# State-space decays as a product of running sums, and the stage's Pool work on DVE

## The chip, the cores and the metric

The kernel runs on one core of one Trainium2 chip. What is measured is the device time of one launch in microseconds. Of the kernel before there are three runs: 1285.94, 1286.4 and 1287.54 us, median 1286.4 us. The engines are called PE (matmul; PEld is its weight load), DVE (vector), ACT (scalar), POOL and SP, which issues most DMAs.

## The reference, cut to what matters

Two transformer blocks over 256 tokens of width 1024. The second block has a sparse attention, a state-space (SSD) branch and a mixture of experts. The change lies in the SSD branch, and there in the decay between two tokens of one chunk:

```python
dt = softplus(dt_raw + dt_bias); A = -exp(a_log)
a_cs = cumsum(dt * A)                        # along the tokens of a chunk
seg = a_cs[:, :, :, None] - a_cs[:, :, None, :]
decay = exp(where(causal, seg, -inf))        # one per head, token l, token s <= l
cb = einsum('bclgn,bcsgn->bclsg', C, B)
y_diag = einsum('bclsg,bclsgr,bcsgrp->bclgrp', cb, decay, x * dt)
...
y = y_diag + y_off + d_skip[:, None] * x
```

There are 32 heads of width 64 in 4 groups of 8.

## The kernel before

Everything is unrolled in one program. In order of time: a feed-forward layer and a mixer (to about 400 us), the second feed-forward layer (to about 600 us), a gated input (`ple`), then `block2` (about 640 to 1022 us), the routing (to about 1050 us) and the experts, whose weights stream in until the end. Large products are made of three fp32r matmuls each (`mm3`, L207 to L209; `xbc`, L1023 to L1025): every weight tile arrives by DMA as `raw`, ACT rounds it to `hi` (L190) and DVE takes the rest `lo = raw - hi` (L191). So each weight tile costs ACT and DVE an instruction before PE can use it.

The kernel's tiles work on two halves of 128 tokens (t = 0, 1), and the SSD chunk here is such a half. `block2` first makes the attention, and `steps` (L1050) the step sizes `dt` and `da = dt * A` (128 tokens x 2 halves x 32 heads), with `das`, `da` split into two fp32r parts (L1066, L1067). `overlaps` (L1075) makes the products of B and C, masked by `tri`. Then `ssd` (L1128) runs over eight units (g, t), and `weave` (L1210) puts steps of a filler between its parts: the `xbc` products of the next groups with their convolutions (`conv_pair`, L982, whose taps are DVE instructions at L991 and L999), the gates and the attention's output product. Per unit:

- `weights(g, t)` (L1086): POOL scales the triangle `tri` by each of 8 heads' `das`, once for each part, giving two tiles `ra` of 128 x 1024 (L1091). PE multiplies them by `upper_r` (L1097, L1098), which sums `da` between two tokens, for 4 heads at a time into one PSUM bank; ACT takes the exponential into `M` (L1099) and DVE multiplies by the masked overlaps (L1100). DVE makes `xdt` (L1105); POOL makes the skip term `ys` (L1106) and, for t = 0, `xw` (L1110).
- `take(g, t)` (L1112): for t = 1 the product with the state (L1118), scaled by DVE (`yo`, L1120) and added to `y` by POOL (L1121); the 16 matmuls of `M` and `xdt` (L1125) and the sum on DVE (L1126).
- `gated(g, t)` (L1144): the gate and a normalisation, whose power is taken on POOL (`rstd`, L138) between DVE instructions (L136, L140, L141, L143).

Each engine runs its own list of instructions in order. The lists of PE, DVE, ACT and SP are set by a planner before the launch, which follows the program's order as a priority and takes later instructions ahead where their inputs are there (`steps` runs at 665 us on DVE, for instance). POOL's list is the program's order (`manual_schedule`), so a normalisation's power stands behind the `ra` of the unit that the program names before it. Work tiles come from pools of slots by size (25 of 4 KB a partition, 7 of 2 KB, 8 of 1 KB); a tile waits for a free slot.

`block2_consts` (L817) has its first part after the mixer, with the masks on POOL, its second in the middle of the last products of the second feed-forward layer (`between`, about 592 us), where DVE copies `upper` to `upper_r` (L837).

Of the kernel before, what the change touches and what calls it, by code (L numbers as in the profile page):

```python
# [54 lines left out]
def tile_blocks(ctx, tc, a, out):  # L55
# [43 lines left out]
    def bc(ap, shape):  # L99
        return ap.to_broadcast(shape)  # L100
# [716 lines left out]
    def block2_consts():  # L817
        cs2 = cp.tile([128, 2, 2, 8], F32, name="cs2")
        sn2 = cp.tile([128, 2, 2, 8], F32, name="sn2")
        for t in range(2):  # L820
            G.dma_start(cs2[:, t].rearrange("p j d -> p (j d)"), a["c_cos2"][t * 128:(t + 1) * 128, :])
            G.dma_start(sn2[:, t].rearrange("p j d -> p (j d)"), a["c_sin2"][t * 128:(t + 1) * 128, :])
        g_q = row_bcast(a["q_norm_2"], 64, "g_q2")
        g_k = row_bcast(a["k_norm_2"], 64, "g_k2")
        g_ik = row_bcast(a["idx_k_norm_2"], 64, "g_ik2")
        b_dt = row_bcast(a["dt_bias_2"], 32, "b_dt")
        a_neg = row_bcast(a["a_log_2"], 32, "a_neg")
        d_row = row_bcast(a["d_skip_2"], 32, "d_row")
        tri = select_mask(F32, "tri", (1.0, 0.0), ALU.is_ge, 0, -1, 1)
        upper = select_mask(F32, "upper", (1.0, 0.0), ALU.is_gt, 0, 1, -1)  # L830

        cw_in = heap([120, 128], name="cw_in")
        G.dma_start(cw_in[:96, :], a["conv_w_2"].rearrange("j (b f) -> (j b) f", f=128))
        G.dma_start(cw_in[96:120, :], a["conv_b_2"].rearrange("(b f) -> b f", f=128))
        yield
        upper_r = cp.tile([128, 128], FR, name="upper_r")
        keep(V.tensor_copy(upper_r, upper))  # L837
        cw = cp.tile([128, 5, 24], F32, name="cw")
        p = tp()
        keep(PE.transpose(p[:, 0, :120], cw_in, ident[:120, :120]))  # L840
        V.tensor_scalar(cw.rearrange("p j b -> p (j b)"), p[:, 0, :120], 0.5, None, op0=ALU.mult)
        keep(S.activation(a_neg, a_neg, AF.Exp))
        V.tensor_scalar(a_neg, a_neg, -1.0, None, op0=ALU.mult)
        wn = heap([128, 8, 104], name="wn")
        for c0, n0, n in ((0, 2048, 72), (72, 7240, 32)):
            nc.sync.dma_start(wn[:, :, c0:c0 + n], w_src(a["w_in_2"], 0, 8, n0, n))
        yield
        wh, wl = heap([128, 8, 104], FR, name="wnh"), heap([128, 8, 104], FR, name="wnl")
        keep(S.copy(wh, wn))
        V.tensor_tensor(wl, wn, wh.bitcast(F32), op=ALU.subtract)  # L850
        yield cs2, sn2, g_q, g_k, g_ik, b_dt, a_neg, d_row, tri, upper, upper_r, cw, wh, wl

    def block2(x, px, consts, done):
        w_in = a["w_in_2"]
        cs2, sn2, g_q, g_k, g_ik, b_dt, a_neg, d_row, tri, upper, upper_r, cw, wh, wl = consts

        sx = px.x

# [174 lines left out]
        dtx = small([128, 2, 32], name="dtx")  # L1033
        dt = small([128, 2, 32], name="dt")
        da = small([128, 2, 32], name="da")
        das = [small([128, 2, 32], FR, name="das") for _ in range(2)]

        def narrow():

# [6 lines left out]
                yield True  # L1046

        dec = small([128, 2, 32], name="dec")

        def steps():  # L1050

            e, s2, pl = [small([128, 2, 32], name="sps") for _ in range(3)]
            V.scalar_tensor_tensor(e, dtx, -1.0, dtx, op0=ALU.mult, op1=ALU.min)
            S.activation(e, e, AF.Exp)
            V.tensor_scalar(pl, e, 2.0, None, op0=ALU.add)
            V.reciprocal(pl, pl)
            V.tensor_tensor(e, e, pl, op=ALU.mult)
            V.tensor_tensor(s2, e, e, op=ALU.mult)
            V.tensor_scalar(pl, s2, 1.0 / 17, None, op0=ALU.mult)
            for n in (15, 13, 11, 9, 7, 5, 3):  # L1060
                V.scalar_tensor_tensor(pl, pl, 1.0 / n, s2, op0=ALU.add, op1=ALU.mult)
            V.scalar_tensor_tensor(pl, pl, 1.0, e, op0=ALU.add, op1=ALU.mult)
            V.tensor_scalar(dtx, dtx, 0.0, None, op0=ALU.max)
            V.scalar_tensor_tensor(dt, pl, 2.0, dtx, op0=ALU.mult, op1=ALU.add)
            V.tensor_tensor(da, dt, bc(a_neg[:, None, :], [128, 2, 32]), op=ALU.mult)
            V.tensor_copy(das[0], da)  # L1066
            V.tensor_tensor(das[1], da, das[0].bitcast(F32), op=ALU.subtract)  # L1067
            pe_ = at((128, 2, 32))
            PE.matmul(pe_[:, 0, :], upper, da[:, 0, :], start=True, stop=False)
            PE.matmul(pe_[:, 1, :], tri, da[:, 1, :], start=False, stop=True)  # L1070
            S.activation(dec, pe_, AF.Exp)
# [14 lines left out]
        def weights(g, t):  # L1086

            hs = slice(g * 8, g * 8 + 8)
            ra = [heap([128, 8, 128], FR, name="ra") for _ in range(2)]
            for i in range(2):  # L1090
                G.tensor_tensor(out=ra[i], in0=bc(tri[:, None, :], [128, 8, 128]),  # L1091
                                in1=bc(das[i][:, t, hs, None].bitcast(F32), [128, 8, 128]), op=ALU.mult)
            M = heap([128, 8, 128], name="M")
            for i in range(2):
                h4 = slice(4 * i, 4 * i + 4)
                ps = at((128, 4, 128))
                PE.matmul(ps, upper_r, ra[0][:, h4, :], start=True, stop=False)  # L1097
                PE.matmul(ps, upper_r, ra[1][:, h4, :], start=False, stop=True)  # L1098
                S.activation(M[:, h4, :], ps, AF.Exp)  # L1099
                V.tensor_tensor(M[:, h4, :], M[:, h4, :], bc(state["cb"][0][:, g, None, t, :], [128, 4, 128]), op=ALU.mult)  # L1100
            if t == 0:
                ys[g] = heap([128, 2, 8, 64], name="y")
            xv = xs[g][:, t, :].rearrange("p (h d) -> p h d", d=64)
            xdt = heap([128, 8, 64], name="xdt")
            V.tensor_tensor(xdt, xv, bc(dt[:, t, hs, None], [128, 8, 64]), op=ALU.mult)  # L1105
            G.tensor_tensor(out=ys[g][:, t], in0=xv, in1=bc(d_row[:, hs, None], [128, 8, 64]), op=ALU.mult)  # L1106
            state[g, t] = M, xdt
            if t == 0:
                xw = state[g] = heap([128, 8, 64], name="xw")
                G.tensor_tensor(out=xw, in0=xdt, in1=bc(dec[:, 0, hs, None], [128, 8, 64]), op=ALU.mult)  # L1110

        def take(g, t):  # L1112
            hs = slice(g * 8, g * 8 + 8)
# [2 lines left out]
            if t == 1:  # L1116
                pof = at((128, 8, 64))
                PE.matmul(pof, state["cb"][1][:, g, :], state[g], start=True, stop=True)  # L1118
                yo = heap([128, 8, 64], name="yo")
                V.tensor_tensor(yo, pof, bc(dec[:, 1, hs, None], [128, 8, 64]), op=ALU.mult)  # L1120
                G.tensor_tensor(out=y, in0=y, in1=yo, op=ALU.add)  # L1121
            py = mm((128, 8, 64), "o")
            for i in range(8):
                for c in (slice(0, 64), slice(64, 128)):
# [553 lines left out]
```

## Time and profile before

| | us |
|---|---|
| median of three runs | 1286.4 |
| the profiled execution | 1286.94 |
| its span in the profile | 1285.2 |
| `block2` with the SSD units | 800 to 970 |
| its last products | 970 to 1022 |
| routing, experts | 1022 to 1285 |

The rows further down are of the profiled execution, whose times run from the span's start. A line number is the line of the kernel that issued the instruction, which can be a helper's. The granted clock (PEclk) is TensorE's share of full speed. Busy times of one engine are joined; idle time of an engine that nobody waits for costs nothing.

### The profile page before, as it was taken

To read this page: it belongs to the slowest core of one execution; us is meant where nothing else is said; L and a number is where in the kernel's file an instruction comes from. 1 tells how busy PE (TensorE), PEld (TensorE's weight loads), DVE (VectorE), ACT (ScalarE), POOL (GpSimd) and SP (SyncE) were. 2 spreads that over 40 slices of the span, in tenths; PEclk is the share of its full clock that TensorE was granted. 3 is DMA by queue.
4 is the path that set the end of the run, shared out by engine and by line. 5 is a ranking of instruction groups with operands and counts; after the bars stand their busy time and mean duration, and the time that the engine had idled before them with its cause. 6 is when DMAs were issued, how large, how long until landed. Compare 5 with 4: busy or idle time off the path is not lost.

```text
span 1285.2 us, 19517 instructions
## 1 busy us (share of the span) xinstructions
PE 1194.2 (93%) x7806; PEld 956.8 (74%) x7807; DVE 759.3 (59%) x1313; ACT 547.6 (43%) x842; POOL 130.9 (10%) x146
## 2 busy tenths in 40 slices
PE   7999999989999999999998899989999979787886
PEld 6999989977777999987777788877778855342421
DVE  5555648675466656646778777998785652121212
ACT  5444535456664444435554666455533321010100
POOL 2000001120002200000001100533430010000000
PEclk9999999999999999999999999999999979999998
DMA  9553655463335654656444244344546859999995
GB/s 335 172 195 121 240 166 169 152 204 136 108 115 169 190 196 141 219 182 193 164 144 151 99 132 134 129 139 124 126 170 214 317 226 391 408 409 408 409 409 201
DMA packets 105567, 266.83 MB, mean 208 GB/s; under 512 B 8580, under 2 KB 15920, under 8 KB 105472
## 3 DMA queue, kind: packets, MB, share of 16 engines
q1 hardware_dynamic: 103488, 260.50, 57.7%
q0 software_dynamic: 1840, 4.52, 1.3%
q8 instruction: 63, 1.03, 0.3%
q10 hardware_dynamic: 144, 0.52, 0.1%
q14 instruction: 32, 0.26, 0.1%
HBM read 264.47 MB, written 1.05 MB: 207 GB/s over the span
## 4 chain that ended last, share of the span: by engine, by line
PE 44%; DMA 13%; DVE 11%; issue 7%; POOL 2%; ACT 1%; SPq 0%; DVEq 0%; POOLq 0%; ACTq 0%
PE mm L207 6%; PE mm L209 6%; PE mm L208 6%; DMA wq<-in_w_up_dram 4%; DVE lo L191 4%; DMA wq<-in_w_down_dram 3%; DMA wq<-in_w_gate_dram 3%; PE mm L261 2%; PE mm L262 2%; PE mm L260 2%; PE at L261 2%; PE at L262 2%; PE at L260 2%; POOL r L138 1%; PE at L1467 1%
## 5 line engine op out<-in xcount | busy, mean ns | idle before, releaser
L191 DVE TENSOR_TENSOR lo<-raw,hi 128x1024 fp32r<-128x1024 f32 (+3 forms) x312 | 374.4, 1205 | 213.2 <-ACT hi L190 209.8
L190 ACT CAST hi<-raw 128x1024 fp32r<-128x1024 f32 (+3 forms) x312 | 315.6, 1015 | 338.6 <-PE o L208 93.8
L138 POOL TENSOR_TENSOR r<-ms,phalf 128x1 f32<-128x1 f32 (+2 forms) x40 | 38.8, 969 | 715.1 <-DVE ms L136 709.9
L1467 PE MATMUL at<-wq,xg 128*32 128x256 f32 x736 | 67.0, 402 | 17.4 <-DMA wq<-in_w_up_dram 13.1
L207 PE MATMUL mm<-hi,xah 128*128 128x512 f32 x192 | 78.8, 410 | 2.9 <-DVE zs L1162 2.9
L209 PE MATMUL mm<-hi,xal 128*128 128x512 f32 x192 | 76.4, 398 | 0.3 <-DVE xal L163 0.3
L208 PE MATMUL mm<-lo,xah 128*128 128x512 f32 x192 | 76.3, 398 | 0.2 <-DVE ms L136 0.2
L1467 PEld LDWEIGHTS at<-wq,xg 128*32 128x32 f32 x736 | 30.0, 114 | 47.9 <-DMA wq<-in_w_up_dram 23.8
L1477 DVE SCALAR_TENSOR_TENSOR act<-at,cg,sa 128x256 f32<-128x256 f32 x8 | 5.3, 666 | 92.6 <-ACT sa L1474 92.5
L1023 PE MATMUL mm<-xah,hi 128*128 128x256 f32 x192 | 56.8, 296 | 3.2 <-ACT sq L892 3.2
L1024 PE MATMUL mm<-xal,hi 128*128 128x256 f32 x192 | 55.0, 286 | 0.0
L1025 PE MATMUL mm<-xah,lo 128*128 128x256 f32 x192 | 55.0, 286 | 0.0
L1474 ACT ACTIVATE sa<-at,rs 128x256 f32<-128x256 f32 x8 | 3.8, 473 | 116.0 <-PE at L1467 77.7
L262 PE MATMUL mm<-x1h,lo 128*128 128x256 f32 x176 | 50.9, 290 | 1.1 <-DVE lo L191 1.1
L261 PE MATMUL mm<-x2l,hi 128*128 128x256 f32 x176 | 50.7, 288 | 1.1 <-DVE x2l L163 1.1
L208 PE MATMUL mm<-lo,gxh 128*128 128x512 f32 x132 | 51.6, 391 | 0.0
L209 PE MATMUL mm<-hi,gxl 128*128 128x512 f32 x132 | 51.5, 390 | 0.0
L260 PE MATMUL mm<-x1h,hi 128*128 128x256 f32 x176 | 51.1, 292 | 0.3 <-ACT x1h L162 0.3
L207 PE MATMUL mm<-hi,gxh 128*128 128x512 f32 x132 | 51.4, 389 | 0.0
L261 PE MATMUL mm<-x1l,hi 128*128 128x256 f32 x176 | 51.0, 291 | 0.0
L262 PE MATMUL mm<-x2h,lo 128*128 128x256 f32 x176 | 50.8, 288 | 0.0
L260 PE MATMUL mm<-x2h,hi 128*128 128x256 f32 x176 | 50.3, 287 | 0.1
(559 smaller groups left out, 3133.6 us busy)
## 6 DMA issues: line engine op xcount, KB each, us to landing
raw<-in_w_in_dram SPq DMA_DIRECT2D x50, 1024.0 KB, 5.0
raw<-in_ffn_w_in_dram SPq DMA_DIRECT2D x40, 1024.0 KB, 5.2
wq<-in_w_down_dram SPq DMA_DIRECT2D x52, 512.0 KB, 10.2
wq<-in_w_up_dram SPq DMA_DIRECT2D x48, 512.0 KB, 10.2
raw<-in_ffn_w_out_dram SPq DMA_DIRECT2D x22, 1024.0 KB, 4.9
wq<-in_w_gate_dram SPq DMA_DIRECT2D x44, 512.0 KB, 10.2
raw<-in_w_gate_dram SPq DMA_DIRECT2D x20, 512.0 KB, 10.2
raw<-in_w_out_dram SPq DMA_DIRECT2D x8, 1024.0 KB, 4.9
```

The source lines that it names most:

```text
L190: first(S.copy(hi, part))
L191: first(V.tensor_tensor(lo, part, hi.bitcast(F32), op=ALU.subtract))
L207: PE.matmul(ps, xh, wh, start=first, stop=False)
L208: PE.matmul(ps, xh, wl, start=False, stop=False)
L209: PE.matmul(ps, xl, wh, start=False, stop=last)
L260: PE.matmul(o, hi[:, c, s], xh, start=(k == 0 and f % 2 == 0), stop=False)
L261: PE.matmul(o, hi[:, c, s], xl, start=False, stop=False)
L262: PE.matmul(o, lo[:, c, s], xh, start=False, stop=end)
L1023: PE.matmul(o, hi[:, c, s], xh, start=(k == 0 and f % 2 == 0), stop=False)
L1024: PE.matmul(o, hi[:, c, s], xl, start=False, stop=False)
L1025: PE.matmul(o, lo[:, c, s], xh, start=False, stop=(k == 7 and f % 2 == 1))
L1467: PE.matmul(pg[s, n * 256:n * 256 + 256], xg[k // 4][:, k % 4, c:c + CAP], ws[j][:, r * 256:r * 256 + 256], start=(n + k == 0), stop=(n + ...
```

## The change

`seg` is a difference of two running sums, and a difference is a product of contraction 2: cs(j) * 1 + 1 * (-cs(i)). The change makes it so. `steps` calls a new function `sums`: DVE repeats each group's 8 heads four times (`rep`, 128 columns), one product per half with `tri` gives 128 rows of running sums by 256 tokens, row 32g + 8k + h holding head h of group g in copy k. ACT and DVE turn the four copies into four parts: copies 0 and 2 are the sum rounded to fp32r, 1 and 3 the rest; in `left` copies 0 and 1 are one and 2 and 3 the negated sum, in `right` the other way round. `right` is 128 x 8 x 128 for each half, zero outside the row's own head (`mine`). `sgn` and `mine` are small constants made in `block2_consts` out of a new identity `eq` on POOL. In `weights`, PE then multiplies 32 rows of `left` by 32 rows of `right`, and adds `m_later` (a very low number where the later token is not later) through `ident_b` in bf16, in place of the two products with `upper_r`. The `ra` tiles, `das` and `upper_r` are gone. The other POOL instructions of `weights` and `take` (L1106, L1110, L1121) become DVE instructions; the power in `rstd` stays on POOL.

```diff
@@ -829,12 +829,31 @@
         tri = select_mask(F32, "tri", (1.0, 0.0), ALU.is_ge, 0, -1, 1)
         upper = select_mask(F32, "upper", (1.0, 0.0), ALU.is_gt, 0, 1, -1)
 
+        m_later = select_mask(BF, "m_later", (0.0, NEG), ALU.is_ge, 0, -1, 1)
+
+        eq = heap([128, 16, 8], name="eq")
+        G.memset(eq, 1.0)
+        for sign in (1, -1):
+            G.affine_select(out=eq, in_=eq, pattern=[[-8 * sign, 16], [-sign, 8]], compare_op=ALU.is_ge, fill=0.0, base=0,
+                            channel_multiplier=sign)
+
         cw_in = heap([120, 128], name="cw_in")
         G.dma_start(cw_in[:96, :], a["conv_w_2"].rearrange("j (b f) -> (j b) f", f=128))
         G.dma_start(cw_in[96:120, :], a["conv_b_2"].rearrange("(b f) -> b f", f=128))
         yield
-        upper_r = cp.tile([128, 128], FR, name="upper_r")
-        keep(V.tensor_copy(upper_r, upper))
+        mine = cp.tile([128, 8], F32, name="mine")
+        keep(V.tensor_reduce(out=mine, in_=eq.rearrange("p a h -> p h a"), axis=AX.X, op=ALU.add))
+        row16, kind = small([128, 16], name="row16"), small([128, 4], name="kind")
+        V.tensor_reduce(out=row16, in_=eq, axis=AX.X, op=ALU.add)
+        V.tensor_reduce(out=kind, in_=row16.rearrange("p (g k) -> p k g", k=4), axis=AX.X, op=ALU.add)
+
+        sgn = cp.tile([128, 5], F32, name="sgn")
+        odd, alt, own, other, minus = [sgn[:, i:i + 1] for i in range(5)]
+        V.tensor_tensor(odd, kind[:, 1:2], kind[:, 3:4], op=ALU.add)
+        V.tensor_scalar(alt, odd, -2.0, 1.0, op0=ALU.mult, op1=ALU.add)
+        V.tensor_tensor(own, kind[:, 0:1], kind[:, 1:2], op=ALU.add)
+        V.tensor_tensor(other, kind[:, 2:3], kind[:, 3:4], op=ALU.add)
+        V.tensor_scalar(minus, other, -1.0, None, op0=ALU.mult)
         cw = cp.tile([128, 5, 24], F32, name="cw")
         p = tp()
         keep(PE.transpose(p[:, 0, :120], cw_in, ident[:120, :120]))
@@ -848,11 +867,11 @@
         wh, wl = heap([128, 8, 104], FR, name="wnh"), heap([128, 8, 104], FR, name="wnl")
         keep(S.copy(wh, wn))
         V.tensor_tensor(wl, wn, wh.bitcast(F32), op=ALU.subtract)
-        yield cs2, sn2, g_q, g_k, g_ik, b_dt, a_neg, d_row, tri, upper, upper_r, cw, wh, wl
+        yield cs2, sn2, g_q, g_k, g_ik, b_dt, a_neg, d_row, tri, upper, m_later, mine, sgn, cw, wh, wl
 
     def block2(x, px, consts, done):
         w_in = a["w_in_2"]
-        cs2, sn2, g_q, g_k, g_ik, b_dt, a_neg, d_row, tri, upper, upper_r, cw, wh, wl = consts
+        cs2, sn2, g_q, g_k, g_ik, b_dt, a_neg, d_row, tri, upper, m_later, mine, sgn, cw, wh, wl = consts
 
         sx = px.x
 
@@ -1033,7 +1052,6 @@
         dtx = small([128, 2, 32], name="dtx")
         dt = small([128, 2, 32], name="dt")
         da = small([128, 2, 32], name="da")
-        das = [small([128, 2, 32], FR, name="das") for _ in range(2)]
 
         def narrow():
 
@@ -1046,6 +1064,28 @@
                 yield True
 
         dec = small([128, 2, 32], name="dec")
+        seg = {}
+
+        def sums():
+
+            odd, alt, own, other, minus = [sgn[:, i:i + 1] for i in range(5)]
+            rep = heap([128, 2, 4, 4, 8], name="rep")
+            for t in range(2):
+                V.tensor_copy(rep[:, t], bc(da[:, t, :].rearrange("p (g h) -> p g h", g=4)[:, :, None, :], [128, 4, 4, 8]))
+            ps = at((128, 256))
+            for t in range(2):
+                PE.matmul(ps[:, tok(t)], rep[:, t].rearrange("p g k h -> p (g k h)"), tri, start=(t == 0), stop=(t == 1))
+            hi, part = heap([128, 256], FR, name="cshi"), heap([128, 256], name="cspart")
+            S.copy(hi, ps)
+            S.activation(part, ps, AF.Identity, scale=odd)
+            x = heap([128, 256], FR, name="cs")
+            V.scalar_tensor_tensor(x, hi.bitcast(F32), alt, part, op0=ALU.mult, op1=ALU.add)
+            left = seg["left"] = heap([128, 256], FR, name="left")
+            V.tensor_scalar(left, x.bitcast(F32), minus, own, op0=ALU.mult, op1=ALU.add)
+            V.tensor_scalar(part, x.bitcast(F32), own, other, op0=ALU.mult, op1=ALU.add)
+            for t in range(2):
+                right = seg[t] = heap([128, 8, 128], FR, name="right")
+                V.tensor_tensor(right, bc(part[:, None, tok(t)], [128, 8, 128]), bc(mine[:, :, None], [128, 8, 128]), op=ALU.mult)
 
         def steps():
 
@@ -1063,8 +1103,7 @@
             V.tensor_scalar(dtx, dtx, 0.0, None, op0=ALU.max)
             V.scalar_tensor_tensor(dt, pl, 2.0, dtx, op0=ALU.mult, op1=ALU.add)
             V.tensor_tensor(da, dt, bc(a_neg[:, None, :], [128, 2, 32]), op=ALU.mult)
-            V.tensor_copy(das[0], da)
-            V.tensor_tensor(das[1], da, das[0].bitcast(F32), op=ALU.subtract)
+            sums()
             pe_ = at((128, 2, 32))
             PE.matmul(pe_[:, 0, :], upper, da[:, 0, :], start=True, stop=False)
             PE.matmul(pe_[:, 1, :], tri, da[:, 1, :], start=False, stop=True)
@@ -1086,16 +1125,13 @@
         def weights(g, t):
 
             hs = slice(g * 8, g * 8 + 8)
-            ra = [heap([128, 8, 128], FR, name="ra") for _ in range(2)]
-            for i in range(2):
-                G.tensor_tensor(out=ra[i], in0=bc(tri[:, None, :], [128, 8, 128]),
-                                in1=bc(das[i][:, t, hs, None].bitcast(F32), [128, 8, 128]), op=ALU.mult)
+            rows = slice(32 * g, 32 * g + 32)
             M = heap([128, 8, 128], name="M")
             for i in range(2):
                 h4 = slice(4 * i, 4 * i + 4)
                 ps = at((128, 4, 128))
-                PE.matmul(ps, upper_r, ra[0][:, h4, :], start=True, stop=False)
-                PE.matmul(ps, upper_r, ra[1][:, h4, :], start=False, stop=True)
+                PE.matmul(ps, seg["left"][rows, tok(t)], seg[t][rows, h4, :], start=True, stop=False)
+                PE.matmul(ps, ident_b, bc(m_later[:, None, :], [128, 4, 128]), start=False, stop=True)
                 S.activation(M[:, h4, :], ps, AF.Exp)
                 V.tensor_tensor(M[:, h4, :], M[:, h4, :], bc(state["cb"][0][:, g, None, t, :], [128, 4, 128]), op=ALU.mult)
             if t == 0:
@@ -1103,11 +1139,11 @@
             xv = xs[g][:, t, :].rearrange("p (h d) -> p h d", d=64)
             xdt = heap([128, 8, 64], name="xdt")
             V.tensor_tensor(xdt, xv, bc(dt[:, t, hs, None], [128, 8, 64]), op=ALU.mult)
-            G.tensor_tensor(out=ys[g][:, t], in0=xv, in1=bc(d_row[:, hs, None], [128, 8, 64]), op=ALU.mult)
+            V.tensor_tensor(ys[g][:, t], xv, bc(d_row[:, hs, None], [128, 8, 64]), op=ALU.mult)
             state[g, t] = M, xdt
             if t == 0:
                 xw = state[g] = heap([128, 8, 64], name="xw")
-                G.tensor_tensor(out=xw, in0=xdt, in1=bc(dec[:, 0, hs, None], [128, 8, 64]), op=ALU.mult)
+                V.tensor_tensor(xw, xdt, bc(dec[:, 0, hs, None], [128, 8, 64]), op=ALU.mult)
 
         def take(g, t):
             hs = slice(g * 8, g * 8 + 8)
@@ -1118,7 +1154,7 @@
                 PE.matmul(pof, state["cb"][1][:, g, :], state[g], start=True, stop=True)
                 yo = heap([128, 8, 64], name="yo")
                 V.tensor_tensor(yo, pof, bc(dec[:, 1, hs, None], [128, 8, 64]), op=ALU.mult)
-                G.tensor_tensor(out=y, in0=y, in1=yo, op=ALU.add)
+                V.tensor_tensor(y, y, yo, op=ALU.add)
             py = mm((128, 8, 64), "o")
             for i in range(8):
                 for c in (slice(0, 64), slice(64, 128)):
```

## Rows read from the trace of the kernel before

**Rows 1.** The head of the page

```profile
...
span 1285.2 us, 19517 instructions
...
```

**Rows 2.** Windows by stage: PE, PEld, DVE, ACT, POOL busy, PEclk, DMA, GB/s

```profile
800.00:970.00 170.00, 157.61 (x1067) 130.50 (x1067) 148.54 (x194) 86.80 (x137) 68.71 (x47) 0.98 0.46 140
970.00:1022.00 52.00, 52.00 (x242) 42.71 (x240) 28.42 (x31) 19.74 (x23) 0.00 (x0) 1.00 0.69 249
1022.00:1062.00 40.00, 33.16 (x316) 25.33 (x317) 21.21 (x77) 9.02 (x21) 6.15 (x6) 0.79 0.67 261
1062.00:1285.00 223.00, 180.24 (x1294) 77.75 (x1286) 46.34 (x90) 17.67 (x32) 0.00 (x0) 0.95 0.96 376
```

**Rows 3.** POOL groups, 800 to 970: count, busy us, mean ns, idle before

```profile
L1091 POOL TENSOR_TENSOR ra<-tri,das 128x1024 fp32r<-128x1024 f32 x16 | 34.2, 2148 | 25.6 <-PE mm L209 13.5 <-PE at L1098 6.9 <-DVE xdt L1105 4.3
L1106 POOL TENSOR_TENSOR y<-xs,d_row 128x512 f32<-128x512 f32 x8 | 13.8, 1719 | 21.7 <-issue 15.7 <-DVE lo L191 6.0
```

**Rows 4.** Groups of DVE and ACT in the same stretch

```profile
L191 DVE TENSOR_TENSOR lo<-raw,hi 128x1024 fp32r<-128x1024 f32 x43 | 59.6, 1400 | 7.3 <-ACT hi L190 6.8 <-PE o L209 0.4
...
L991 DVE SCALAR_TENSOR_TENSOR conv<-pre,cw,conv 128x255 f32<-128x255 f32 (+2 forms) x36 | 19.6, 599 | 0.1
...
L1100 DVE TENSOR_TENSOR M<-M,cbm 128x512 f32<-128x512 f32 x16 | 16.3, 1055 | 0.6 <-ACT M L1099 0.6
...
L140 DVE SCALAR_TENSOR_TENSOR u<-r 128x1 f32<-128x1 f32 x8 | 9.2, 1148 | 2.8 <-POOL r L138 2.8
L1099 ACT ACTIVATE M<-at 128x512 f32<-128x512 f32 x16 | 8.9, 593 | 9.4 <-PE at L1098 9.4
...
L1126 DVE TENSOR_TENSOR y<-o,y 128x512 f32<-128x512 f32 x8 | 5.5, 687 | 4.5 <-POOL y L1121 3.8 <-PE o L1125 0.8
```

**Rows 5.** DVE groups by shape in 980-1022 (two), 690-800 and 598-612

```profile
L191 DVE TENSOR_TENSOR lo<-raw,hi 128x1024 fp32r<-128x1024 f32 x12 | 14.6, 1224 | 10.0 <-ACT hi L190 10.0
L1218 DVE TENSOR_TENSOR gate<-gate,gate 128x512 f32<-128x512 f32 x4 | 2.6, 685 | 0.0
...
L991 DVE SCALAR_TENSOR_TENSOR conv<-pre,cw,conv 128x254 f32<-128x254 f32 x12 | 5.6, 478 | 0.1
...
L140 DVE SCALAR_TENSOR_TENSOR u<-r 128x1 f32<-128x1 f32 x2 | 0.3, 158 | 1.4 <-POOL r L138 1.4
```

**Rows 6.** Waits, 800 to 970: waiter, releaser, us in total, times, longest

```profile
PE tp L1005 <- DVE conv L999: 6.7, 3, 4.0
...
PE o L533 <- DVE probT L518: 2.0, 1, 2.0
```

**Rows 7.** Timeline, 856 to 865: start, us, what, idle before and releaser

```profile
856.55 4.17 POOL L1091 TENSOR_TENSOR ra<-tri,das 128x1024 fp32r<-128x1024 f32 x2
856.85 4.15 DVE L991 SCALAR_TENSOR_TENSOR conv<-pre,cw,conv 128x253 f32<-128x253 f32 x2
...
864.03 1.11 PE L1005 MATMUL tp<-ident,conv 128*128 128x128 f32 x4 [4.05 <-DVE conv L999]
```

**Rows 8.** Windows of single stretches in the stage

```profile
836.00:842.00 6.00, 4.78 (x38) 4.40 (x37) 6.00 (x14) 4.89 (x9) 0.00 (x0) 1.00 0.54 178
...
864.00:868.00 4.00, 3.97 (x12) 3.29 (x13) 4.00 (x10) 3.46 (x7) 0.75 (x1) 0.50 0.79 262
868.00:872.00 4.00, 4.00 (x27) 3.07 (x26) 2.41 (x5) 1.95 (x4) 0.00 (x0) 0.78 0.00 0
```

**Rows 9.** PE groups: L1097 in 800-970, L482 in 724-760

```profile
L1097 PE MATMUL at<-ra,upper_r 128*128 128x512 f32 x16 | 6.2, 426 | 1.0 <-POOL ra L1091 1.0
...
L482 PE MATMUL at<-madd,ident_b 128*128 128x512 bf16 x4 | 1.2, 384 | 0.0
```

**Rows 10.** Timeline of DVE and POOL around 595 us

```profile
594.97 1.43 DVE L353 SCALAR_TENSOR_TENSOR h<-mm,rh,h 128x512 f32<-128x512 f32 x2 [2.54 <-PE mm L209]
...
597.95 0.57 POOL L138 TENSOR_TENSOR r<-ms,phalf 128x1 f32<-128x1 f32 x1 [173.34 <-DVE ms L136]
```

**Rows 11.** Waits of SP from 1000 us to the end

```profile
SPq L1291 <- PE at L1467: 23.4, 10, 19.0
```

## The prediction

> **What bounds the kernel now.** The page gives a span of 1285.2 us [rows 1]; the profiled execution took 1286.94 us, 0.5 above the median of 1286.4. I read the windows by stage first [rows 2]. From 970 to 1022 us PE is busy all the time, and from 1062 us to the end the DMA engines are (share 0.96). The stage that the change touches, 800 to 970, is of neither kind: PE works 157.6 of 170 us and so waits 12.4, while DVE works 148.5 and POOL 68.7. So what a change of this stage can win is PE's waiting, not DVE's or POOL's time as such.
>
> Next I asked the waits of that stage who PE waits for [rows 6]. The two large entries name DVE: 6.7 us in three waits for L999, the last instruction of a convolution, and 2.0 us for a copy of the attention's weights. The timeline of the longest shows the pattern [rows 7]: POOL makes two `ra` in 4.17 us, two taps at L991 take 4.15 us beside them, and PE waits 4.05 us for the convolution's end. Then the cost goes on: the granted clock is 0.50 (the level of 1.2 GHz) from 864 to 868 and 0.78 on average from 868 to 872 [rows 8], after that wait; at 2.4 GHz the same work would have taken 4 x 0.50 + 4 x 0.22 = 2.9 us less.
>
> Is DVE merely full, or slowed? The groups of DVE answer [rows 4] against the same shapes where POOL runs no `ra` [rows 5]: L191 1400 against 1224 ns, the taps 599 against 478, L1100 1055 against 685 (L1218, the same shape), L140 1148 against 158. What reads one input from PSUM isn't slowed: L1126 takes 687. So four groups lose 43 x 0.176 + 36 x 0.121 + 16 x 0.370 + 8 x 0.990 = 7.6 + 4.4 + 5.9 + 7.9 = 25.8 us of DVE time beside POOL's work.
>
> By the Trainium skill (SBUF — State Buffer, "Who interferes with whom") a DVE instruction with two SBUF inputs and a POOL instruction that reads SBUF exclude each other for the whole instruction, and a DVE instruction with one SBUF input isn't touched. L1126 agrees with the second half. By the first, all 68.7 us of POOL could be lost to DVE; the rows show 25.8, and I go by these.
>
> **The change, part by part.** *POOL.* Sixteen `ra` (34.2 us) and eight skip terms (13.8) leave POOL [rows 3], and with them the four `xw` and four sums of half an `ra`'s size. What stays in the stage is the power of the normalisations.
>
> *DVE.* It gets back the 25.8 us. It takes over 16 instructions of 128 x 512 (8 `ys`, 4 `xw`, 4 sums) at 0.685 [rows 5]: 11.0 us. `sums` adds two of 128 x 1024 at 1.22 (2.4) and three of 128 x 256, at most 0.69 and, being half as wide as that row, some 0.35 each (1.0). The copies into `rep` have their input as early as `das` has now, at 665 us, and are as small as the two instructions that go; I put them at nothing, and at under 0.7 us if DVE is full there. Net: 148.5 - 25.8 + 14.4 = 137 us. DVE stays the second busiest engine but is 11 us lighter, and what goes lies where PE waits, while what comes is spread over eight units.
>
> *PE.* 32 products of 512 columns go and 32 come. The 16 with `m_later` are of the form of L482, 384 ns against 426 for L1097 [rows 9]. The 16 with 32 rows have no row here. Bounds: as dear as L1097 and as much again (+6.8 us), or free beside their neighbours (-6.8). I take the nearest row, L1097 itself, whose columns are the same 512: no difference, so nothing for the exchange.
>
> *ACT.* Sixteen exponentials as before; two evictions of 256 columns more, under 0.59 each by L1099 [rows 4].
>
> *The chain in front of the first unit.* Now the first `ra` are made on POOL from 803 us and PE uses them at 815. In the changed kernel the products of `sums` come behind the last attention unit, as L1069 does; then ACT twice, DVE twice (`cs`, `part`) and `right`. With 256 columns at half of the rows of 512: PE 0.4, ACT 0.6, DVE 0.7 and 1.2, with hand-overs some 3.3 us. Whether PE has filler then (the `xbc` products of group 0 stand beside it) decides what shows: nothing at the least, and with the queues of ACT and DVE in front of each step, perhaps 7. I take 3.3, as if nothing hid it.
>
> *Constants.* POOL makes four or five more masks after the mixer; it is idle for 173 us before 597.95 [rows 10], which hides them; without that cover they would be some 2 us. DVE gets eight small instructions (some 1.7 us) near 592, in place of one. It is idle for 2.54 us before 594.97 waiting for PE [rows 10], which hides them; without it, 1.5 us.
>
> *Slots.* The two `right` hold two of the 25 large slots through the stage; the passing pairs of `ra`, one of which had to wait 13.5 us for a slot [rows 3], are gone. No cost.
>
> *What comes behind.* PE works without a pause until 1022, so what the stage gains starts the routing sooner. The expert weights stop in front of the first expert product (SP waits up to 19.0 us for L1467 [rows 11]), so their stream is held by PE there and moves along with it: one to one.
>
> **The sum**, against 1286.94: the waits for L999, -6.7; the one for the copy, -2.0; PE's wait for `ra`, -1.0 [rows 9]; the low clock after the long wait, -2.9; the chain, +3.3. That is -9.3: 1277.6 for the profiled execution, and 0.5 less for the median: **1277**. All of PE's waiting and the low clock together are 12.4 + 2.9 = 15.3, so 1271 is the floor without help from the 32-row products.
>
> **The rivals.**
>
> *A: DVE is full by itself (slower).* From 836 to 842 DVE is busy 6.00 of 6.00 with POOL at 0.00, and PE waits there too (4.78 of 6.00) [rows 8]: no relief is to be had in that place, and the change puts more on DVE. A group's new instructions are 4 x 0.685 = 2.7 us. If the relief falls where nobody waits and the additions in front of the convolutions' ends, the price is 2.7 us in each of the three groups whose `xbc` is made in the stage, 8.2; the chain's 3.3; and one more wait long enough for the low clock, 2.9. Against it stand 4.05 + 2.9 of the long wait, whose cause is plainly `ra`, and 1.0. That is +14.4 - 8.0 = +6.4: 1293. It decides once more than the relief of the long wait is lost again. For it: DVE is busy 87% of the stage, and its order changes. Against it: the net load falls.
>
> The Trainium skill has a rule on this side (Perfetto Trace Analysis, "Optimizing Scalar/DVE Operations"): if DVE is saturated, offloading some work even to GPSIMD may make sense, which here would leave the 16 instructions where they are; the same sentence doubts it for these two engines, as they share a read port. By its first half A's time is right, by its second the forecast's; the rows of L191 and L1100 speak for the second.
>
> *B: the relief is given back (about no change).* The products of `sums` come late, PE runs out of filler around 815 and waits as long as it did before 864, with the low clock behind it: 4.05 + 2.9 = 7.0 instead of the chain's 3.3 alone, and the copy's 2.0 stays: -9.3 + 3.7 + 2.0 = -3.6 and, if one of the two shorter waits for L999 (6.7 - 4.0 = 2.7, half of it 1.4) stays too, -2.2: 1284 to 1285. For it: all lists are planned anew, and `sums` puts five DVE instructions in one place. Against it: the filler of group 0 is there.
>
> *C: POOL was not what slowed DVE.* If L191 and L1100 are slow for another reason, the 14.4 us come and nothing goes; this would be A with a higher price. The timeline of `ra` and L991 side by side [rows 7] leaves it little; it is counted with A.
>
> **How the numbers follow.** A measurement of this kernel tells a difference of about 0.2%, 2.6 us, from none. The forecast (1271 to 1282) has a chance of 0.62, B (1282 to 1288) 0.20, A with C 0.18. B lies on both sides of the bound of 2.6 us at 1283.8: half of it is faster. Faster 0.62 + 0.10 = 0.72; same 0.10 and a little of A, 0.12; slower 0.16. The range takes the forecast and B and leaves out most of A: 1288 above. Below, the floor of 1271 and a little for the 32-row products: 1270.
>
> **What would show it.** In the changed kernel's trace POOL should be busy some 7 to 12 us in the stage (68.7 - 34.2 - 13.8, less eight instructions of 1.0 to 1.7); L191 near 1225 ns, L1100 near 690, the taps near 480, L140 near 160; DVE some 137 us in a stage of about 160; PE's waits for L999 gone or small, and no half clock near 864. The first product of the new form would come between 813 and 822. The time from 970's counterpart to the end should be the same 315 us. I'd be wrong if PE's waits for DVE are as long with DVE's instructions at their quiet lengths (A), if a new long wait stands in front of the first unit (B), or if the 32-row products run far from 0.43 us.

## The result, and the profile after

The changed kernel takes 1272.75 us (median of four runs, 1271.29 to 1274.12) against 1286.17 of the kernel before beside it: a ratio of 0.9894, 95% interval 0.9877 to 0.9911. That is 13.4 us less; the forecast was 1277 us, in a range from 1270 to 1288. The profiled execution of the changed kernel took 1273.31 us, its span is 1271.5.

The windows of the changed kernel by stage, with the columns of [rows 2]; the stage that ended at 970 us now ends at 958:

```profile
800.00:958.00 158.00, 157.88 (x1078) 129.08 (x1078) 132.49 (x216) 88.74 (x139) 8.28 (x15) 1.00 0.49 155
958.00:1010.00 52.00, 52.00 (x244) 42.77 (x242) 27.94 (x34) 19.98 (x24) 0.56 (x1) 1.00 0.69 248
1010.00:1048.00 38.00, 30.85 (x321) 23.86 (x324) 20.38 (x74) 8.28 (x18) 5.58 (x5) 0.87 0.68 259
1048.00:1271.00 223.00, 179.82 (x1280) 77.50 (x1270) 46.28 (x90) 17.68 (x32) 0.00 (x0) 0.93 0.95 376
```

The gain is in the first line. PE worked 157.6 of 170 us there and now works 157.9 of 158: it waits for nothing. DVE went from 148.5 to 132.5 us although it does more, POOL from 68.7 to 8.3. The last line has its old length, and the two between were 52 and 40 us and are 52 and 38 with windows cut at whole microseconds. That the gain is passed on one to one shows in SP's first load of expert weights, first before, then after:

```profile
1000.40 0.34 SPq L1291 DMA_DIRECT2D raw<-in_w_up_dram  x1
```

```profile
986.59 0.34 SPq L1327 DMA_DIRECT2D raw<-in_w_up_dram  x1
```

13.8 us sooner, and the span is 13.7 shorter. I use the time of this load below as the mark of the stage's end.

The groups of the changed kernel that answer to [rows 3 to 5] (L1010 was L991, L1136 was L1100, L1162 was L1126):

```profile
L191 DVE TENSOR_TENSOR lo<-raw,hi 128x1024 fp32r<-128x1024 f32 x44 | 53.6, 1222 | 14.8 <-ACT hi L190 13.3 <-PE at L1154 1.5
...
L1010 DVE SCALAR_TENSOR_TENSOR conv<-pre,cw,conv 128x255 f32<-128x255 f32 (+2 forms) x36 | 15.2, 478 | 1.6 <-ACT conv L1008 1.4
...
L1136 DVE TENSOR_TENSOR M<-M,cbm 128x512 f32<-128x512 f32 x16 | 10.7, 687 | 0.9 <-ACT M L1135 0.9
...
L1162 DVE TENSOR_TENSOR y<-o,y 128x512 f32<-128x512 f32 x8 | 5.5, 686 | 0.0
...
L138 POOL TENSOR_TENSOR r<-ms,phalf 128x1 f32<-128x1 f32 x8 | 4.6, 580 | 34.0 <-DVE ms L136 33.9
...
L140 DVE SCALAR_TENSOR_TENSOR u<-r 128x1 f32<-128x1 f32 x8 | 1.3, 157 | 2.8 <-POOL r L138 2.7
```

Each of the four DVE groups that the prediction called slowed has its quiet length, the one it has where POOL runs no `ra`: 1222 ns where it was 1400 (1224 quiet), 478 for 599, 687 for 1055, 157 for 1148. L1162, with one input from PSUM, has the 686 ns that it had. And the clock where the long wait was, columns as in [rows 8]:

```profile
860.00:880.00 20.00, 20.00 (x121) 15.70 (x120) 19.54 (x36) 15.25 (x25) 0.56 (x1) 1.00 0.41 143
```

DVE is 19.5 of 20 us busy there, more than anywhere else in the stage, and still PE is never without work, at a granted clock of 1.00.

### The profile page after: what moved, and what is told of

It reads as the page before. It is cut to its first block, busy times and chain, and to the rows that moved or that the text cites. A ratio compares the mean times of both kernels' runs of the same rounds, so it can differ in the third digit from the quotient of the medians.

```text
span 1271.5 us, 19511 instructions
## 1 busy us (share of the span) xinstructions
PE 1193.3 (94%) x7810; PEld 956.3 (75%) x7811; DVE 743.0 (58%) x1341; ACT 549.9 (43%) x844; POOL 73.0 (6%) x119
## 4 chain that ended last, share of the span: by engine, by line
PE 47%; DMA 13%; DVE 8%; issue 6%; POOL 1%; ACT 1%; SPq 0%; DVEq 0%; POOLq 0%; ACTq 0%
PE mm L207 6%; PE mm L208 6%; PE mm L209 6%; DMA wq<-in_w_up_dram 4%; DMA wq<-in_w_down_dram 4%; DMA wq<-in_w_gate_dram 3%; DVE lo L191 2%; PE mm L1042 2%; PE mm L1044 2%; PE mm L1043 2%; PE mm L261 2%; PE mm L262 2%; PE mm L260 2%; PE at L262 2%; PE at L261 2%
## 5 line engine op out<-in xcount | busy, mean ns | idle before, releaser
L191 DVE TENSOR_TENSOR lo<-raw,hi 128x1024 fp32r<-128x1024 f32 (+3 forms) x312 | 367.2, 1181 | 220.1 <-ACT hi L190 215.6
```

Of the source, the lines that this page charges most:

```text
L191: first(V.tensor_tensor(lo, part, hi.bitcast(F32), op=ALU.subtract))
```

## The experiments

Two theories are told apart first. *Sharing*: DVE's instructions last longer while POOL reads beside them, and PE waits for DVE. *Waiting*: POOL's results themselves came late, and the length of DVE's instructions did not matter. Then: which half of the change does it, is DVE near its limit, and what bounds the stage now. "Load" is the start of the first load of expert weights; "PE waits" is 170 us less PE's busy time from 800 to 970, for the changed kernel 158, and for e6 and e8 to e10 155 us from 800. Each ratio is taken to runs of the kernel before made beside the run, so runs are compared by their ratios.

| run | median us | ratio to before (95%) | load at | PE waits |
|---|---|---|---|---|
| before | 1286.4 | | 1000.40 | 12.4 |
| changed | 1272.75 | 0.9894 (0.9877 to 0.9911) | 986.59 | 0.1 |
| e1_ghost_ra | 1289.51 | 1.0024 (1.0013 to 1.0034) | 1001.74 | 10.7 |
| e2_ghost_write | 1272.13 | 0.9884 (0.9868 to 0.9901) | 985.80 | 0.1 |
| e4_products_only | 1277.24 | 0.9927 (0.9911 to 0.9944) | 990.64 | 3.2 |
| e5_small_only | 1283.29 | 0.9972 (0.9962 to 0.9982) | 997.79 | 9.6 |
| e3_ra_on_dve | 1273.97 | 0.9893 (0.9876 to 0.9909) | 988.34 | 2.9 |
| e7_dve_more | 1275.12 | 0.9908 (0.9891 to 0.9925) | 987.25 | 0.8 |
| e10_changed_again | 1272.47 | 0.9892 (0.9877 to 0.9907) | 986.40 | 0.1 |
| e6_abs_for_mask | 1270.04 | 0.9877 (0.9862 to 0.9892) | 984.55 | 1.3 |
| e8_rows_128 | 1271.73 | 0.9879 (0.9861 to 0.9897) | 984.25 | 0.9 |
| e9_both | 1265.78 | 0.9846 (0.9832 to 0.9859) | 979.32 | 1.8 |

### POOL reads that nobody needs

The triangles are made on POOL again, into a tile that nobody reads:

```diff
             sums()
+            seg["ghost"] = heap([128, 8, 128], name="ghost")
...
             rows = slice(32 * g, 32 * g + 32)
+            for i in range(2):
+                G.tensor_tensor(out=seg["ghost"], in0=bc(tri[:, None, :], [128, 8, 128]),
+                                in1=bc(da[:, t, hs, None], [128, 8, 128]), op=ALU.mult)
```

> The changed kernel, with the sixteen triangle products on POOL put back into a tile that nobody reads; all else as changed. Sharing (DVE's instructions last longer beside POOL's reads, and PE waits for DVE): POOL some 42 us busy in the stage, L191 back to 1350 to 1400 ns and the taps to 560 to 600, DVE some 20 to 25 us busier, PE's waits in the stage back to 6 to 12 us: 1280 to 1287 us. Waiting (PE and DVE stood behind POOL's results; the length of DVE's instructions did not matter): nobody waits for these tiles, so 1272 to 1275 us.

It takes 1289.51 us: all that the change brought is lost, and 3 us more. That is 2.5 us above the range that sharing gave, with less stretching than it gave (L191 at 1311 ns, not 1350 to 1400). Of this run the window of the stage (columns of [rows 2]), the groups of DVE and POOL in it, three of its waits, and stretches with a lower clock:

```profile
800.00:970.00 170.00, 159.26 (x1068) 129.40 (x1067) 154.12 (x216) 87.36 (x140) 44.26 (x31) 0.98 0.46 139
```

```profile
L191 DVE TENSOR_TENSOR lo<-raw,hi 128x1024 fp32r<-128x1024 f32 x43 | 56.0, 1311 | 7.7 <-ACT hi L190 7.7
...
L1131 POOL TENSOR_TENSOR ghost<-tri,da 128x1024 f32<-128x1024 f32 x16 | 33.9, 2119 | 0.8
...
L1010 DVE SCALAR_TENSOR_TENSOR conv<-pre,cw,conv 128x255 f32<-128x255 f32 (+2 forms) x36 | 18.3, 566 | 1.3 <-ACT conv L1008 1.2
...
L1140 DVE TENSOR_TENSOR M<-M,cbm 128x512 f32<-128x512 f32 x16 | 12.9, 825 | 1.2 <-ACT M L1139 1.1
...
L1166 DVE TENSOR_TENSOR y<-o,y 128x512 f32<-128x512 f32 x8 | 5.5, 684 | 0.0
```

```profile
PE tp L1024 <- DVE conv L1018: 4.4, 2, 2.2
...
PE o L533 <- DVE probT L518: 2.8, 1, 2.8
...
PE at L1121 <- ACT cbo L1123: 1.7, 1, 1.7
```

```profile
812.00:816.00 4.00, 2.71 (x17) 2.38 (x18) 3.96 (x6) 0.00 (x0) 3.84 (x3) 0.70 0.41 158
...
866.00:870.00 4.00, 1.86 (x7) 1.68 (x8) 4.00 (x8) 1.80 (x5) 0.00 (x0) 0.77 0.33 83
870.00:874.00 4.00, 4.00 (x18) 3.30 (x17) 3.55 (x6) 3.11 (x5) 3.23 (x3) 0.80 0.46 179
```

Nobody waits for POOL here, and yet L191 is at 1311, the taps at 566, L1140 at 825 ns; L1166, with its PSUM input, keeps 684. DVE is 154 us busy, and PE waits for the same two things as in [rows 6]: a convolution's end and the attention's copy. Behind such waits the granted clock is 0.70 to 0.80 in the stretches shown. Waiting alone would have left 1272 to 1275. The 3 us more than before come in part from the chain of `sums`, which now runs beside the first triangles: PE's wait of 1.7 us at 820 us, for a product of B and C that DVE masks behind that chain, is not among PE's waits in the kernel before. The chain's two instructions of 128 x 256 with one tensor input, in the timeline of DVE:

```profile
814.11 1.87 DVE L1084 TENSOR_SCALAR left<-cs,sgn 128x256 fp32r<-128x256 f32 x1
815.90 2.05 DVE L1085 TENSOR_SCALAR cspart<-cs,sgn 128x256 f32<-128x256 f32 x1
```

They took 0.41 us each in the changed kernel.

### POOL writes that nobody needs

The same place, with fills instead of products:

```diff
+            for i in range(4):
+                G.memset(seg["ghost"], float(i))
```

> As the one before, but POOL fills the unread tile with a constant (64 fills of 128x1024 in place of the 32 products' halves: four a unit), so that it is busy and writes, and reads nothing. Sharing through reads: L191 stays near 1225 ns and the time at 1272 to 1275 us. Sharing through any access, or a normalisation's power standing behind other POOL work as the cause: as with the triangle products, 1279 us or more. Waiting: 1272 to 1275 us.

(Four a unit are 32 fills, not the 64 of that text.) 1272.13 us, as the changed kernel. Window and groups of this run:

```profile
800.00:970.00 170.00, 169.88 (x1131) 139.12 (x1130) 137.66 (x219) 93.03 (x142) 40.68 (x47) 1.00 0.51 158
```

```profile
L191 DVE TENSOR_TENSOR lo<-raw,hi 128x1024 fp32r<-128x1024 f32 x49 | 59.7, 1221 | 21.5 <-ACT hi L190 21.4
...
L1131 POOL MEMSET ghost<- 128x1024 f32 x32 | 30.7, 958 | 1.5
...
L1139 DVE TENSOR_TENSOR M<-M,cbm 128x512 f32<-128x512 f32 x16 | 10.6, 686 | 1.6 <-ACT M L1138 1.5
```

POOL is 40.7 us busy, nearly as long as with the triangles (44.3), and the powers stand behind its fills as they stood behind the triangles. DVE's lengths are the quiet ones, PE waits for nothing. So it is not that POOL is busy, nor the order of its list: it is that it reads. By the Trainium skill (SBUF — State Buffer, "Who interferes with whom") a DVE instruction with two SBUF inputs contends with a POOL instruction that reads SBUF and not with one that only writes it; these two runs agree, at 1311 and 1221 ns for L191.

### One half of the change at a time

Products only: `ys`, `xw` and the sum of `y` stay on POOL. Small only: the triangles stay, and these three move.

```diff
# e4_products_only, against the changed kernel
-            V.tensor_tensor(ys[g][:, t], xv, bc(d_row[:, hs, None], [128, 8, 64]), op=ALU.mult)
+            G.tensor_tensor(out=ys[g][:, t], in0=xv, in1=bc(d_row[:, hs, None], [128, 8, 64]), op=ALU.mult)
...
-                V.tensor_tensor(y, y, yo, op=ALU.add)
+                G.tensor_tensor(out=y, in0=y, in1=yo, op=ALU.add)
# e5_small_only, against the kernel before: the same lines the other way round
```

> Half of the change: the product of running sums, with the skip terms, xw and the sums of y left on POOL (some 25 us there). Sharing: DVE is 11 us lighter than in the changed kernel and loses some 25/69 of 25.8 = 9 us again; PE's waits some 0 to 3 us: 1272 to 1277 us. Waiting: DVE waits for POOL's sums of y again (3.8 us before), PE behind it: 1275 to 1280 us. If most of the gain comes from the sixteen moved instructions: 1282 us or more.

> The other half: the triangles stay on POOL, the sixteen smaller instructions go to DVE. Sharing: POOL keeps 34 of its 59 us of reading work, DVE keeps some 15 us of the 25.8 lost and gets 11 more: about as before, 1282 to 1290 us. Waiting: POOL's queue is shorter, the triangles come sooner and nobody waits for the sums of y: 1276 to 1282 us.

The products alone give 0.9927, the small ones 0.9972. Together 0.9894: the two gains, 0.73 and 0.28%, are nearly the whole. The groups that tell why, first of e4, then of e5:

```profile
L191 DVE TENSOR_TENSOR lo<-raw,hi 128x1024 fp32r<-128x1024 f32 x47 | 58.0, 1240 | 24.4 <-ACT hi L190 22.9 <-PE at L1154 1.5
...
L1146 POOL TENSOR_TENSOR xw<-xdt,dec 128x512 f32<-128x512 f32 x4 | 7.4, 1859 | 11.8 <-DVE xdt L1141 11.8
...
L1162 DVE TENSOR_TENSOR y<-o,y 128x512 f32<-128x512 f32 x8 | 5.5, 686 | 4.6 <-POOL y L1157 4.5
```

```profile
L191 DVE TENSOR_TENSOR lo<-raw,hi 128x1024 fp32r<-128x1024 f32 x44 | 57.8, 1324 | 11.9 <-ACT hi L190 10.4 <-PE at L1098 1.5
...
L1091 POOL TENSOR_TENSOR ra<-tri,das 128x1024 fp32r<-128x1024 f32 x16 | 35.2, 2219 | 30.0 <-PE mm L208 15.7 <-PE at L1098 6.1 <-DVE xdt L1105 4.2
...
L1100 DVE TENSOR_TENSOR M<-M,cbm 128x512 f32<-128x512 f32 x16 | 14.3, 925 | 4.2 <-ACT M L1099 4.2
```

In e4 there is little sharing left (L191 1240), and what it lacks to the changed kernel is more of the other kind: DVE waits 4.5 us for POOL's sum of `y` (L1162), POOL's `xw` take 1859 ns each, and PE's one long wait, 2.3 us before 859.87, stands at the end of a chain that begins with such a sum (2.73 us on POOL from 851.75; the clock is 0.67 from 860 to 864 after it). In the same chain L140 takes 0.99 us beside POOL's skip term (157 ns quiet), so sharing is not absent there. So waiting has its part in the small instructions, and the time, 1277.24, lies in the range that waiting gave and just above that of sharing. In e5 the triangles remain and with them the long DVE instructions (1324, 925), and the time lies in the range of sharing alone.

### Is DVE the next limit, and is the product form needed?

The triangles on DVE in the kernel before, with the three small ones, and no running sums; and 16 unread products of 128 x 1024 more on DVE in the changed kernel:

```diff
# e3_ra_on_dve, against the kernel before; the three small ones as in e5
-                G.tensor_tensor(out=ra[i], in0=bc(tri[:, None, :], [128, 8, 128]),
-                                in1=bc(das[i][:, t, hs, None].bitcast(F32), [128, 8, 128]), op=ALU.mult)
+                V.tensor_tensor(ra[i], bc(tri[:, None, :], [128, 8, 128]),
+                                bc(das[i][:, t, hs, None].bitcast(F32), [128, 8, 128]), op=ALU.mult)
# e7_dve_more, against the changed kernel, twice a unit
+            V.tensor_tensor(seg["ghost"], bc(tri[:, None, :], [128, 8, 128]), bc(da[:, t, hs, None], [128, 8, 128]), op=ALU.mult)
```

> The kernel before with all of the stage's POOL work but the powers on DVE, the triangles included, and without the product of running sums: DVE gets 16 x 1.22 = 19.5 us for the triangles and 11.0 for the sixteen smaller ones, some 150 of 158 us. If the product form is only a way to get the triangles off POOL and DVE has room to 95%: 1272 to 1276 us. If DVE is the bound by then (rival A's place): PE waits for convolutions and for the triangles, 1277 to 1287 us.

> The changed kernel with 16 instructions of 128x1024 more on DVE whose result nobody reads (two a unit, 19.5 us): DVE some 152 of 158 us. Room left: 1271 to 1275 us. DVE as the bound: PE's waits for DVE come back, by at least what does not fit into DVE's 25 idle us at the places where it is full, 1277 to 1287 us. A theory by which only DVE's busy share counts puts this run and the one before within 2 us of each other.

The windows of the stage, e3 and then e7, and between them the triangles of e3:

```profile
800.00:970.00 170.00, 167.13 (x1125) 140.43 (x1125) 151.45 (x232) 91.42 (x144) 10.53 (x15) 0.99 0.50 153
```

```profile
L1091 DVE TENSOR_TENSOR ra<-tri,das 128x1024 fp32r<-128x1024 f32 x16 | 19.2, 1219 | 0.1
```

```profile
800.00:970.00 170.00, 169.19 (x1124) 137.78 (x1123) 152.87 (x234) 90.73 (x141) 12.00 (x15) 1.00 0.51 156
```

e3 has the ratio of the changed kernel, 0.9893: with the small ones moved as well, taking the triangles off POOL is the rest of the gain, and the product of running sums is one way to do it, which leaves DVE 13 us lighter (132.5 against 145.5 us from 800 to 958). e7 is 0.9908, and its interval overlaps that of the changed kernel (0.9892 in e10); its 1275.12 us lie just above the range for room left and under that for DVE as the bound. Its load starts 0.7 to 0.9 us later, and some 1.8 us later if counted from PE's last work in front of the stage (L482 starts at 790.6 us there, at 791.8 in the changed kernel). DVE at 151 to 153 of 170 us, busier than in the kernel before (148.5), makes PE wait 2.9 and 0.8 us where it waited 12.4. The plainest pair is e1 and e7: DVE is busy 154 and 153 us, and the times lie 14 us apart. DVE's busy share was not what PE paid for; the stretched instructions in a few places were. Why 19.5 us of added instructions find places that do no harm and 17 us of stretching don't was not tested.

### What bounds the stage now

With PE at 157.9 of 158 us only less work on PE, or the same work at a lower price, can help. Two edits, alone and together, beside the changed kernel on one chip:

```diff
# e6_abs_for_mask
-                PE.matmul(ps, seg["left"][rows, tok(t)], seg[t][rows, h4, :], start=True, stop=False)
-                PE.matmul(ps, ident_b, bc(m_later[:, None, :], [128, 4, 128]), start=False, stop=True)
-                S.activation(M[:, h4, :], ps, AF.Exp)
+                PE.matmul(ps, seg["left"][rows, tok(t)], seg[t][rows, h4, :], start=True, stop=True)
+                S.activation(M[:, h4, :], ps, AF.Abs)
+                S.activation(M[:, h4, :], M[:, h4, :], AF.Exp, scale=-1.0)
# e8_rows_128, band being one for the rows of group g
+            seg["left"] = heap([128, 4, 256], FR, name="left4")
+            for g in range(4):
+                V.tensor_scalar(seg["left"][:, g, :], left, band[:, g:g + 1], None, op0=ALU.mult)
...
-                PE.matmul(ps, seg["left"][rows, tok(t)], seg[t][rows, h4, :], start=True, stop=False)
+                PE.matmul(ps, seg["left"][:, g, tok(t)], seg[t][:, h4, :], start=True, stop=False)
```

> The changed kernel without the sixteen products with m_later: where the later token is not later the difference is positive, so ACT takes the absolute value and then the exponential of its negative, and no mask is needed. ACT gets 16 x 0.6 = 9.6 us more (89 to 98 of 158). If the stage is now bound by PE's work: 16 products of 0.18 to 0.23 us from start to next start go, and what they leave behind may be dearer, -1 to -3.7 us: 1269 to 1272 us. If the stage is bound by DVE or ACT: no change or slower, 1272.5 us or more.

> The changed kernel with all 128 rows of the running sums in each product, the rows of other groups made zero in four copies of left (DVE some 2 us more, once). A product of 32 rows takes 0.43 us from its start to the next start on PE, the one of 128 rows before took 0.26. If the 32 rows are the reason and PE bounds the stage: 16 x 0.17 = -2.7 us, 1269 to 1271 us. If it is the change of operands, or PE does not bound the stage: 1272 to 1275 us.

> Both of the two before. PE bounds the stage: the sum of both gains, 1266 to 1270 us. Otherwise 1272 us or more.

> The changed kernel as it is, beside the three before it: 1271 to 1274 us by every theory.

The price of the products, in the timelines of PE: the kernel before, the changed kernel, e9.

```profile
814.87 0.28 PE L1024 MATMUL mm<-xal,hi 128*128 128x256 f32 x1
814.99 0.45 PE L1097 MATMUL at<-ra,upper_r 128*128 128x512 f32 x1
815.28 0.39 PE L1098 MATMUL at<-ra,upper_r 128*128 128x512 f32 x1
815.51 0.28 PE L1025 MATMUL mm<-xah,lo 128*128 128x256 f32 x1
815.62 0.28 PE L1023 MATMUL mm<-xah,hi 128*128 128x256 f32 x1
```

```profile
817.78 0.28 PE L1043 MATMUL mm<-xal,hi 128*128 128x256 f32 x1
817.99 0.49 PE L1133 MATMUL at<-right,left 32*128 32x512 f32 x1
818.41 0.39 PE L1134 MATMUL at<-m_later,ident_b 128*128 128x512 bf16 x1
818.45 0.47 PE L1044 MATMUL mm<-xah,lo 128*128 128x256 f32 x1
818.76 0.28 PE L1042 MATMUL mm<-xah,hi 128*128 128x256 f32 x1
```

```profile
817.69 0.73 PE L1138 MATMUL at<-right,left 128*128 128x512 f32 x2
818.25 0.28 PE L1045 MATMUL mm<-xal,hi 128*128 128x256 f32 x1
```

Before, two products and one of 256 columns (0.12 us) lie between 814.99 and 815.62: 0.51 us for the pair. In the changed kernel it is 817.99 to 818.76: 0.65, and 0.42 pass from the product of 32 rows to its successor. The product in front of the pair is followed after 0.21 us, not 0.12 as before; with this the pair costs 0.74. In e9 two products without masks take 817.69 to 818.25: 0.28 each. Over all 16 pairs, from each product's start to the next start on PE (waits taken off), the mean is 0.52 us a pair before, 0.61 in the changed kernel, 0.41 in e8, which changes nothing but the rows, and 0.27 for the one product of e9.

e6 gives 1270.04 and e9 1265.78 beside 1272.47; e8's 1271.73 can't be told from the changed kernel by its time (its runs lie from 1268.34 to 1272.01), but its load starts 2.2 us sooner, as e6's does by 1.9. Both together bring 7.1 us by that mark, more than 4.1. Part of this lies ahead of the stage: PE's last products of queries and keys in front of it (L479) start at 788.76 us in e9, and at 791.18, 790.68 and 790.42 in e6, e8 and e10. From there to the load e6 is 2.6 us shorter than e10, e8 2.4 and e9 5.4, which is nearly the sum. The window of e9 shows that PE is still the bound, with waits of 1.8 us:

```profile
800.00:955.00 155.00, 153.24 (x1073) 129.50 (x1072) 132.48 (x219) 95.27 (x152) 10.89 (x15) 1.00 0.53 161
```

e9_both is the fastest version found: 0.9846 of the kernel before.

## Why the prediction was right

The sum's terms, one by one:

- *The waits for L999 (-6.7) and for the copy (-2.0), PE's wait for `ra` (-1.0), the low clock (-2.9)*: all gone, the first two and the low clock for the reason given: e1 brings them back (4.4 and 2.8 us of waits) with nothing but POOL's products, and e2, with POOL's fills, doesn't. The wait for `ra` went with the `ra`.
- *The other 2.7 us of PE's 12.4* were left standing in the sum as waits without a cause I could price. They went too: PE waits 0.1 us.
- *The chain of `sums` (+3.3)* is the term that was most wrong. The chain itself took longer than 3.3 us, near the 7 that the prediction gave as its upper end. The timeline of the changed kernel:

```profile
807.92 0.61 PE L1077 MATMUL at<-tri,rep 128*128 128x128 f32 x4
...
811.45 1.22 DVE L1088 TENSOR_TENSOR right<-cspart,mine 128x1024 fp32r<-128x1024 f32 x1
...
813.19 1.22 DVE L1088 TENSOR_TENSOR right<-cspart,mine 128x1024 fp32r<-128x1024 f32 x1
```

From the first product at 807.9 to the end of the second `right` are 6.5 us, and the first product of the new form starts at 817.99. But PE had the filler that the prediction named and then didn't count: the `xbc` products of group 0 and the overlaps. A chain costs what PE lacks meanwhile, and it lacked nothing.
- *The 32-row products (0 within ±6.8)* cost 0.74 - 0.51 = 0.23 us a pair at the place shown, 16 x 0.23 = 3.7 us, an estimate from that one place. The bounds held; the row taken was too cheap.

So -15.3 (all waiting and the low clock) + 3.7 = -11.6, against 13.6 between the two profiled executions (1286.94 and 1273.31): 2 us of gain are in none of the terms. A sum over PE's timeline from 790 us to the load shows on which side they lie. PE's work, from start to start, was 197.7 us and its waits 12.4 before; it is 196.3 us of work and no wait now. So the work fell by 1.4 us: 2.9 by the clock, of which the dearer products and all else took back only 1.5. Part of the 2 us is that a wait costs more than the idle time put down to it: in the kernel before, the product at 859.60 runs its 0.39 us to the end in front of the long wait, where others of its shape are followed after 0.23, and there were eleven waits. The rest wasn't traced.

The time came out 4 us under the forecast of 1277, near the floor of 1271, inside the range. That the main term was right is no luck; that the time fell so near the floor is in part: the chain and the other 2.7 us, counted as lost, erred one way and the products the other.

Rival A priced DVE as the bound. Where DVE is fullest, 19.5 of 20 us in the changed kernel's window from 860 to 880, PE doesn't wait; and 19.5 us more in e7 cost some 2. The rival's own row was DVE full from 836 to 842 without POOL. In the changed kernel DVE is as full there (6.00 of 6.00), and PE works all 6.00. That the row was the tail of a queue that POOL's reads had stretched between 803 and 827 is likely, and no run shows it by itself. Of what the Trainium skill says (Perfetto Trace Analysis, "Optimizing Scalar/DVE Operations"), which is two sentences there, the second is borne out, the doubt about two engines that share a read port: DVE did 14.4 us more and became 16 us lighter. Rival B (PE out of filler around 815) did not come; its own sum, -3.6 to -2.2 and 0.5 off, gives 1282.8 to 1284.2, not 1284 to 1285.

The 25.8 us of stretched DVE time, 14.4 us of additions and 137 us of DVE work were right within 5 (132.5 in a stage of 158). The 4.5 us are about what smaller groups lost too, which the prediction left out: the product `xdt` (L1105 before, L1141 now) went from 852 to 685 ns, L141 from 360 to 155. The prediction also took too wide what the Trainium skill says of one SBUF input (SBUF — State Buffer, "Who interferes with whom"): it says so outside the two-port modes only, and in e1 two instructions with one tensor input were stretched.

## What to carry to other kernels

When DVE instructions with two SBUF inputs are longer in one stage than in another at the same shape, look for POOL reading beside them before counting either engine's busy share; a copy of POOL's work whose result nobody needs shows about the price in one run (here 17 us, some 3 of them new). Moving such work to DVE can make DVE lighter. And a new serial chain costs only what the bounding engine lacks in that time: name its filler and count it, or leave the chain out of the sum.

## What the runs showed of the hardware that was not expected

- A DVE instruction with a single tensor input and per-partition scalars (128 x 256) took 1.87 and 2.05 us beside POOL's triangles (e1), 0.41 in the changed kernel. So it isn't only instructions with two tensor inputs that POOL's reads stretch; which property of these two does it was not tested.
- POOL's fills (958 ns each, 32 of them, e2) left DVE's instructions at their quiet lengths (L191 1221 ns).
- A product of 32 rows and 512 columns kept PE 0.42 us until the next product started, where one of 128 rows before took 0.29 in the same place; fewer rows were dearer. In e9 the same product with 128 rows, most of them zero, took 0.28, and in e8, where only the rows differ, a pair takes 0.41 us where it took 0.61.
